# Two of the three matmuls of w_up's split product joined into one of 512 columns, and their halves added by VectorE

## The chip, the cores and the metric

The kernel runs on one core of a Trainium2 chip. The time is the device time of one execution in microseconds; a lower one is better. The runs before the change gave 347.18, 345.4 and 346.83 us, median 346.83. One more execution was profiled: it took 347.6 us, and every row below is from it.

## What is computed

One layer of a decoder with 256 tokens and 1024 features, in fp32: a norm, one projection to q, k and v, two groups of attention heads, an output projection with a residual, then the squared-relu MLP that the change touches, then a gated embedding and a last norm. Cut to what matters here:

```python
D_MODEL, SEQ, D_FF = 1024, 256, 4 * 1024

hn = rmsnorm(h, g_mlp[i])
h = h + jnp.square(jax.nn.relu(hn @ w_up[i])) @ w_down[i]     # w_up (1024, 4096), w_down (4096, 1024)
gate = jax.nn.sigmoid(rmsnorm(h, g_ple[i]) @ w_ple_gate[i] + b_ple_gate[i])
h = h + gate * (p[i] @ w_ple_proj[i])
```

## The kernel before

**Split products.** Each large product is done in fp32r, a format that TensorE takes at the rate of one column per cycle, with both operands split in two: hi is the operand rounded to fp32r by ScalarE (`ACTIVATE Copy`), lo is the operand less hi, by VectorE. A product a·b is then three matmuls into the same PSUM bank, hi·hi, hi·lo and lo·hi. The helper `mm3` (lines 149 to 153) issues them: L151 hi·hi, L152 stationary hi with moving lo or the other way round, L153 the last. Since `mm3` is used everywhere, the lines L151 to L153 carry most of the program's matmuls; the tiles in a row tell the stage: `ps<-hhi,hi` and `ps<-hlo,hi` are the up projection (activations h hi and lo, weights hi and lo), `ps<-hi,u` and `ps<-lo,u` the down projection (u are the activations of the MLP), `ps<-hi,p` the embedding.

**Units.** The program is a list of units, each with its weights (two slabs of 1 MB) and its steps. `run_units` (L109) issues the loads two units ahead on SP's queue, and in the steps of one unit the splits of the next unit's weights: eight pieces of 512 columns for w_up (L75 ScalarE hi, L76 VectorE lo, which also multiply by the norm's gain) and four of 1024 columns for w_down (L83, L84). The scheduler of the language then sets the order of each engine's queue.

**The MLP.** Up unit u (`up_steps`, L588) makes 512 of the 4096 hidden features for all 256 tokens: four blocks c of 128 features, each a sum over eight k of 128 input features. Stationary is a 128x128 block of the weights, moving are the 256 tokens, so one (c, k) is three matmuls of 256 columns, and a unit has 32 of these steps, 96 matmuls. Down unit u (`dn_steps`, L627) multiplies the 512 hidden features with 512 rows of w_down: 16 steps, 48 matmuls of 512 columns, summed over all eight units in four PSUM banks that stay held from the first to the last. The order is up 0, embedding, up 1, down 0, up 2, down 1, ..., up 7, down 6, down 7. Up unit 0 goes over the first four k for all blocks and then over the last four, because the features of its second half are transposed late; the others go block by block.

**The evacuation** of an up block (`act`, L576): relu out of PSUM on ScalarE (L581), the square on GpSimd (L583), hi on ScalarE (L585), lo on VectorE (L586). It works on two blocks (512 columns, one bank) at a time, in unit 0 on one (256 columns).

**The activations.** `act_pair` (L164) gives a tile for hi and one for lo, each with 8 k of 256 tokens; `to_features` (L515) fills them from transposes: hi by ScalarE (L523), lo by VectorE (L524).

Of the kernel before, what the change touches and what calls it, by code (L numbers as in the profile page):

```python
# [10 lines left out]
F32 = mybir.dt.float32  # L11
F32R = mybir.dt.float32r
BF16 = mybir.dt.bfloat16
AF = mybir.ActivationFunctionType
ALU = mybir.AluOpType
PSUM = bass.MemoryType.PSUM

P = 128
S = 256
DM = 1024  # L20
KT = DM // P
# [11 lines left out]
def block_kernel(ctx: ExitStack, tc: tile.TileContext, a: dict):  # L33
    nc = tc.nc

    outer = ctx.enter_context(tc.tile_pool(name="outer", bufs=1))
# [6 lines left out]
    def bank():  # L43
        n_ps[0] += 1
        return psum.tile([P, 512], F32, tag="ps", name=f"ps{n_ps[0]}")
# [103 lines left out]
    def mm3(ps, lhs, rhs, start, stop):  # L149

        nc.tensor.matmul(ps, lhs[0], rhs[0], start=start, stop=False)  # L151
        nc.tensor.matmul(ps, lhs[0], rhs[1], start=False, stop=False)  # L152
        last_mm[0] = nc.tensor.matmul(ps, lhs[1], rhs[0], start=False, stop=stop)  # L153

    last_mm = [None]
# [6 lines left out]
        nc.tensor.matmul(wps[:, :P], warm, warm, start=True, stop=True)  # L162

    def act_pair(name):  # L164
        hi = outer.tile([P, KT, S], F32R, tag="aThi", name=name + "hi")
        lo = outer.tile([P, KT, S], F32R, tag="aTlo", name=name + "lo")
        return hi, lo

    h_sb = outer.tile([P, 2, DM], F32, name="h_sb")
    stat = outer.tile([P, 64], F32, name="stat")  # L170
# [23 lines left out]

    xT = ap.tile([P, KT, S], F32, tag="xy", name="xT")
    aT = act_pair("x")
    x_rows = lambda k0, k1: xT[:, k0:k1] if k0 else head[:, 4 * KT :].unsqueeze(1)

# [340 lines left out]
    def alloc_aT2():  # L539
        state["aT2"] = act_pair("h")  # L540
# [6 lines left out]
    aT2 = Lazy("aT2")  # L547
# [13 lines left out]
    uT = {}  # L561

    def open_mlp():
        attn_pool.__exit__(None, None, None)
        mp["p"] = ctx.enter_context(tc.tile_pool(name="mlp", bufs=1))
        m = mp["p"]
        mp["ple"] = m.tile([P, 2, DM], F32, name="ple")
        mp["bg"] = m.tile([P, 2, DM], F32, name="bg")
        nc.sync.dma_start(mp["bg"], bass.AP(tensor=a["bg"].tensor, offset=a["bg"].offset, ap=[[0, P], [DM, 2], [1, DM]]))
        pT = m.tile([P, 2, S], F32, name="pTin")  # L570
        nc.sync.dma_start(pT, a["pT"])
        mp["p2"] = [m.tile([P, 2, S], F32R, name=f"p2{i}") for i in range(2)]
        nc.scalar.activation(mp["p2"][0], pT, AF.Copy)
        nc.vector.tensor_tensor(mp["p2"][1], pT, mp["p2"][0].bitcast(F32), op=ALU.subtract)

    def act(u, q, ps, c):  # L576

        m = mp["p"]
        w = c * S
        r = m.tile([P, w], F32, tag=f"r{c}", name="r", bufs=2)  # L580
        nc.scalar.activation(r, ps[:, :w], AF.Relu)  # L581
        sq = m.tile([P, w], F32, tag=f"sq{c}", name="sq", bufs=2)
        nc.gpsimd.tensor_tensor(sq, r, r, op=ALU.mult)  # L583
        o = [t.rearrange("p c s -> p (c s)")[:, q * S : q * S + w] for t in uT[u]]
        nc.scalar.activation(o[0], sq, AF.Copy)  # L585
        nc.vector.tensor_tensor(o[1], sq, o[0].bitcast(F32), op=ALU.subtract)  # L586

    def up_steps(u):  # L588
        def steps():
            if u == 0:  # L590
                open_mlp()
            uT[u] = [mp["p"].tile([P, 4, S], F32R, tag=f"u{n}", name="u", bufs=3) for n in ("hi", "lo")]

            def one(ps, c, k):
                s = slabs_up[u][k // 4]
                col = slice(c * P, (c + 1) * P)
                mm3(ps, (s.hi[:, k % 4, col], s.lo[:, k % 4, col]), (aT2[0][:, k], aT2[1][:, k]), k == 0, k == KT - 1)

            if u == 0:
                b = [bank() for _ in range(4)]  # L600
                for kk in range(2):
                    for c in range(4):
                        for k in range(4 * kk, 4 * kk + 4):
                            one(b[c][:, :S], c, k)
                            yield
                        if kk:
                            act(u, c, b[c], 1)
            else:
                for cc in range(2):
                    ps = bank()  # L610
                    for c in (2 * cc, 2 * cc + 1):
                        for k in range(KT):
                            one(ps[:, (c % 2) * S : (c % 2 + 1) * S], c, k)
                            yield
                    act(u, 2 * cc, ps, 2)
        return steps

    dn = {}
# [8 lines left out]
    def dn_steps(u):  # L627
        def steps():
            if u == 0:
                dn["ps"] = {(t, n): bank() for t in range(2) for n in range(2)}  # L630

            def one(t, n, c):
                s = slabs_dn[u][c // 2]
                tok, col = slice(t * P, (t + 1) * P), slice(n * 512, (n + 1) * 512)
                mm3(dn["ps"][t, n], (uT[u][0][:, c, tok], uT[u][1][:, c, tok]),
                    (s.hi[:, c % 2, col], s.lo[:, c % 2, col]), u == 0 and c == 0, u == NU - 1 and c == 3)

            if u < NU - 1:
                for c in range(4):
                    for t in range(2):  # L640
                        for n in range(2):
                            one(t, n, c)
                            yield
                return
            state["aT2"] = act_pair("g")
            for t in range(2):
                for n in range(2):
                    for c in range(4):
                        one(t, n, c)
                        yield  # L650
                    col = slice(n * 512, (n + 1) * 512)
                    nc.vector.scalar_tensor_tensor(h_sb[:, t, col], dn["ps"][t, n], dn["r2"][:, t : t + 1],
                                                   h_sb[:, t, col], op0=ALU.mult, op1=ALU.add)
                    defer(3, lambda t=t, n=n: (to_features(aT2, t, n), row_sum(gsum, t, n)))
        return steps
# [145 lines left out]
```

## Time and profile before

| | |
|---|---|
| median of three runs | 346.83 us (345.4 to 347.18) |
| profiled execution | 347.6 us |
| its span, first to last instruction | 345.8 us |
| mean granted clock of TensorE | 0.982 of 2.4 GHz |
| busy: TensorE, VectorE, ScalarE, GpSimd | 96%, 63%, 58%, 21% of the span |
| moved by DMA | 60.87 MB, 176 GB/s |

Matmuls overlap in the records: one of 256 columns is listed with 283 ns, while the next one starts 120 ns after it. What TensorE needs for one is therefore read as the distance of start times. Busy shares are averages over the whole program; the stretches by stage are among the rows below. Where the order of a queue is shown, an engine's instructions stand in their sequence, with the semaphores that they wait for and no times.

### The profile page before, as it was taken

Reading aid. Unit: us, or ns where it says so; the run is one execution under the profiler, and the core shown is the slowest. Engines: PE = TensorE matmul, PEld = TensorE weight load, DVE = VectorE, ACT = ScalarE, POOL = GpSimd, SP = SyncE. Lnnn points to the kernel's source line nnn. Section 1 sums busy time; section 2 is a strip of 40 time slices with the busy share of each in tenths; the row PEclk is TensorE's granted clock in tenths of the full one; section 3 lists DMA queues with packets and bytes.
Section 4 is the critical chain, followed back from the end, with each engine's and each line's share of the span. In section 5 each row is a group of like instructions: output and inputs, shape, how many; then the busy total and the mean of one; then the engine's idle time right before and its main releaser. Section 6 shows DMA issues by size and latency. Waiting matters only on the chain.

```text
span 345.8 us, 5641 instructions
## 1 busy us (share of the span) xinstructions
PE 333.2 (96%) x2188; PEld 298.9 (86%) x2188; DVE 216.8 (63%) x380; ACT 199.8 (58%) x378; POOL 74.1 (21%) x103
## 2 busy tenths in 40 slices
PE   8899899999999999999999999999999999999990
PEld 8699779899877889898998988989989899888890
DVE  4789948687837769537537275292553843758563
ACT  6786838677664668728255374373652825458431
POOL 0025563455214001311020110110201102000443
PEclk9999969999999999999999999999999999999996
DMA  7998951404444369653727618357194463700011
GB/s 193 372 401 289 316 187 53 160 33 159 163 170 159 112 236 321 206 213 115 261 116 248 237 46 320 123 173 263 51 327 159 136 242 110 243 2 1 2 62 61
DMA packets 10971, 60.87 MB, mean 176 GB/s; under 512 B 1216, under 2 KB 1984, under 8 KB 4416
## 3 DMA queue, kind: packets, MB, share of 16 engines
q1 hardware_dynamic: 10944, 60.51, 49.4%
q8 instruction: 17, 0.28, 0.4%
q14 instruction: 10, 0.08, 0.1%
HBM read 59.46 MB, written 1.05 MB: 175 GB/s over the span
## 4 chain that ended last, share of the span: by engine, by line
PE 92%; DMA 2%; POOL 2%; DVE 1%; SPq 1%; ACT 0%; issue 0%; POOLq 0%; DVEq 0%
PE ps L151 29%; PE ps L152 28%; PE ps L153 28%; DMA raw<-in_w_in 2%; PE ps L328 2%; PE ps L371 2%; PE ps L359 2%; PE ps L519 1%; POOL pb L349 1%; SPq L208 1%; PE ps L372 1%; POOL bias L318 1%; DVE lo L76 0%; POOL bias L316 0%; PE ps L271 0%
## 5 line engine op out<-in xcount | busy, mean ns | idle before, releaser
L76 DVE SCALAR_TENSOR_TENSOR lo<-raw,head,hi 128x512 fp32r<-128x512 f32 (+2 forms) x137 | 105.0, 813 | 24.9 <-ACT hi L75 24.6
L75 ACT ACTIVATE hi<-raw,head 128x512 fp32r<-128x512 f32 (+2 forms) x137 | 92.7, 733 | 25.2 <-PE ps L152 11.1
L151 PE MATMUL ps<-hhi,hi 128*128 128x256 f32 x256 | 72.6, 283 | 0.0
L153 PE MATMUL ps<-hhi,lo 128*128 128x256 f32 x256 | 72.5, 283 | 0.0
L152 PE MATMUL ps<-hlo,hi 128*128 128x256 f32 x256 | 72.4, 283 | 0.0
L84 DVE TENSOR_TENSOR lo<-raw,hi 128x1024 fp32r<-128x1024 f32 x34 | 41.5, 1254 | 28.1 <-ACT hi L83 28.0
L583 POOL TENSOR_TENSOR sq<-r 128x512 f32<-128x512 f32 (+1 forms) x18 | 19.9, 1108 | 141.8 <-ACT r L581 141.8
L151 PE MATMUL ps<-hi,u 128*128 128x512 f32 x128 | 50.2, 392 | 0.0
L83 ACT ACTIVATE hi<-raw 128x1024 fp32r<-128x1024 f32 x34 | 34.3, 1052 | 27.2 <-PE ps L153 25.5
L152 PE MATMUL ps<-lo,u 128*128 128x512 f32 x128 | 49.9, 390 | 0.0
L153 PE MATMUL ps<-hi,u 128*128 128x512 f32 x128 | 49.8, 389 | 0.0
L152 PEld LDWEIGHTS ps<-hlo,hi 128*128 128x128 f32 x256 | 49.1, 192 | 0.3
L151 PEld LDWEIGHTS ps<-hhi,hi 128*128 128x128 f32 x256 | 49.1, 192 | 0.3
L153 PEld LDWEIGHTS ps<-hhi,lo 128*128 128x128 f32 x256 | 49.1, 192 | 0.0
L151 PE MATMUL ps<-xhi,hi 128*128 128x256 f32 x128 | 38.7, 303 | 0.0
L152 PE MATMUL ps<-xlo,hi 128*128 128x256 f32 x128 | 36.9, 289 | 0.0
L153 PE MATMUL ps<-xhi,lo 128*128 128x256 f32 x128 | 36.7, 289 | 0.0
L586 DVE TENSOR_TENSOR u<-sq,u 128x512 fp32r<-128x512 f32 (+1 forms) x18 | 11.7, 650 | 34.0 <-ACT u L585 34.0
L153 PEld LDWEIGHTS ps<-hi,u 128*128 128x128 f32 x128 | 24.0, 188 | 5.1
L151 PEld LDWEIGHTS ps<-hi,u 128*128 128x128 f32 x128 | 24.1, 188 | 4.7
L152 PEld LDWEIGHTS ps<-lo,u 128*128 128x128 f32 x128 | 24.1, 188 | 4.7
L151 PEld LDWEIGHTS ps<-xhi,hi 128*128 128x128 f32 x128 | 25.2, 197 | 1.5 <-issue 0.7
(128 smaller groups left out, 531.7 us busy)
## 6 DMA issues: line engine op xcount, KB each, us to landing
raw<-in_w_up SPq DMA_DIRECT2D x16, 1024.0 KB, 5.1
raw<-in_w_down SPq DMA_DIRECT2D x16, 1024.0 KB, 4.8
raw<-in_w_in SPq DMA_DIRECT2D x8, 1024.0 KB, 7.2
raw<-in_w_out SPq DMA_DIRECT2D x4, 1024.0 KB, 4.9
raw<-in_w_gate SPq DMA_DIRECT2D x4, 1024.0 KB, 5.1
raw<-in_w_in SPq DMA_DIRECT2D x4, 512.0 KB, 8.8
raw<-in_w_in SPq DMA_DIRECT2D x7, 256.0 KB, 7.0
h_sb<-in_x SPq DMA_DIRECT2D x1, 1024.0 KB, 7.4
```

The lines of the kernel that those rows point to most:

```text
L75: nc.scalar.activation(h, r, AF.Copy, scale=sc)
L76: nc.vector.scalar_tensor_tensor(l, r, sc, h.bitcast(F32), op0=ALU.mult, op1=ALU.subtract)
L83: nc.scalar.activation(h, r, AF.Copy)
L84: nc.vector.tensor_tensor(l, r, h.bitcast(F32), op=ALU.subtract)
L151: nc.tensor.matmul(ps, lhs[0], rhs[0], start=start, stop=False)
L152: nc.tensor.matmul(ps, lhs[0], rhs[1], start=False, stop=False)
L153: last_mm[0] = nc.tensor.matmul(ps, lhs[1], rhs[0], start=False, stop=stop)
L328: last_mm[0] = nc.tensor.matmul(ps[h][:, c : c + w], d["q"][a_][r, q0 : q0 + P], d["k"][b_][r, :w], start=i == 0, stop=i == 2)
L359: nc.tensor.transpose(ps[:, c * P : (c + 1) * P], d["p"][:, h, c * P : (c + 1) * P], ident)
L371: nc.tensor.matmul(o[:, :S], v[:, 0, cols], d["pT"][h][:, :S], start=True, stop=False)
L583: nc.gpsimd.tensor_tensor(sq, r, r, op=ALU.mult)
L586: nc.vector.tensor_tensor(o[1], sq, o[0].bitcast(F32), op=ALU.subtract)
```

## The change

The two tiles of hi and lo become one tile in which, for each k, the 256 tokens of hi are followed by the 256 of lo; hi and lo are views of it, and a third view has both as 512 columns. A step of an up unit is now two matmuls: the weights' hi with the activations' hi and lo in one matmul of 512 columns over a whole PSUM bank, and the weights' lo with the activations' hi, 256 columns, added into the second half of the bank. The first half of the bank then holds hi·hi and the second half hi·lo and lo·hi. Each block has its bank, so an up unit uses four.

The evacuation goes block by block in all units: ScalarE copies the second half out of PSUM, VectorE adds the first half to it, VectorE does the squared relu in one operation (maximum with 0, times the value), ScalarE makes hi and VectorE lo. GpSimd has no part in it any more.

```diff
     def act_pair(name):
-        hi = outer.tile([P, KT, S], F32R, tag="aThi", name=name + "hi")
-        lo = outer.tile([P, KT, S], F32R, tag="aTlo", name=name + "lo")
-        return hi, lo
+        both = outer.tile([P, KT, 2, S], F32R, tag="aT", name=name)
+        return both[:, :, 0], both[:, :, 1], both.rearrange("p k h s -> p k (h s)")
...
-    def act(u, q, ps, c):
+    def act(u, q, ps):
         m = mp["p"]
-        w = c * S
-        r = m.tile([P, w], F32, tag=f"r{c}", name="r", bufs=2)
-        nc.scalar.activation(r, ps[:, :w], AF.Relu)
-        sq = m.tile([P, w], F32, tag=f"sq{c}", name="sq", bufs=2)
-        nc.gpsimd.tensor_tensor(sq, r, r, op=ALU.mult)
-        o = [t.rearrange("p c s -> p (c s)")[:, q * S : q * S + w] for t in uT[u]]
-        nc.scalar.activation(o[0], sq, AF.Copy)
-        nc.vector.tensor_tensor(o[1], sq, o[0].bitcast(F32), op=ALU.subtract)
+        b = m.tile([P, S], F32, tag="r", name="r", bufs=3)
+        nc.scalar.copy(b, ps[:, S:])
+        z = m.tile([P, S], F32, tag="z0", name="z0", bufs=3)
+        nc.vector.tensor_tensor(z, ps[:, :S], b, op=ALU.add)
+        sq = m.tile([P, S], F32, tag="sq", name="sq", bufs=3)
+        nc.vector.scalar_tensor_tensor(sq, z, 0.0, z, op0=ALU.max, op1=ALU.mult)
+        hi, lo = (t[:, q] for t in uT[u])
+        nc.scalar.activation(hi, sq, AF.Copy)
+        nc.vector.tensor_tensor(lo, sq, hi.bitcast(F32), op=ALU.subtract)
...
             def one(ps, c, k):
                 s = slabs_up[u][k // 4]
                 col = slice(c * P, (c + 1) * P)
-                mm3(ps, (s.hi[:, k % 4, col], s.lo[:, k % 4, col]), (aT2[0][:, k], aT2[1][:, k]), k == 0, k == KT - 1)
...
+                nc.tensor.matmul(ps, s.hi[:, k % 4, col], aT2[2][:, k], start=k == 0, stop=False)
+                last_mm[0] = nc.tensor.matmul(ps[:, S:], s.lo[:, k % 4, col], aT2[0][:, k],
+                                              start=False, stop=k == KT - 1)
+
+            b = [None] * 4
+            for ks in (range(4), range(4, 8)) if u == 0 else (range(8),):
+                for c in range(4):
+                    if ks[0] == 0:
+                        b[c] = bank()
+                    for k in ks:
+                        one(b[c], c, k)
+                        yield
+                    if ks[-1] == KT - 1:
+                        act(u, c, b[c])
```

TensorE at the start of up unit 2, before (h is the activations, hi and lo behind the comma the weights):

```order
L151 MATMUL ps_2019<-hhi,hi 128x256 [waits Activation_49]
L152 MATMUL ps_2019<-hlo,hi 128x256
L153 MATMUL ps_2019<-hhi,lo 128x256 [waits DVE_49]
L151 MATMUL ps_2019<-hhi,hi 128x256 [waits Activation_49]
L152 MATMUL ps_2019<-hlo,hi 128x256
L153 MATMUL ps_2019<-hhi,lo 128x256 [waits DVE_49]
```

and now:

```order
L598 MATMUL ps_1983<-h,hi 128x512 [waits DVE_49,Activation_49]
L599 MATMUL ps_1983<-h,lo 128x256 [waits DVE_49]
L598 MATMUL ps_1983<-h,hi 128x512 [waits Activation_49]
L599 MATMUL ps_1983<-h,lo 128x256 [waits DVE_49]
L598 MATMUL ps_1983<-h,hi 128x512 [waits Activation_49]
```

Three matmuls of a step became two; the wide one waits for ScalarE's hi of the weights, the narrow one for VectorE's lo, as before. VectorE from the splits for down unit 1 (L84) over up unit 2 to the splits for up unit 3 (L76), before:

```order
L84 TENSOR_TENSOR lo<-raw,hi 128x1024 [waits DMAHW5_49,Activation_49]
L84 TENSOR_TENSOR lo<-raw,hi 128x1024 [waits Activation_49]
L586 TENSOR_TENSOR u<-sq,u 128x512 [waits Activation_49]
L76 SCALAR_TENSOR_TENSOR lo<-raw,head,hi 128x512 [waits DMAHW6_49,PE_49,Activation_49]
L76 SCALAR_TENSOR_TENSOR lo<-raw,head,hi 128x512 [waits Activation_49] x3
L76 SCALAR_TENSOR_TENSOR lo<-raw,head,hi 128x512 [waits DMAHW7_49,PE_49,Activation_49]
L586 TENSOR_TENSOR u<-sq,u 128x512 [waits Activation_49]
L76 SCALAR_TENSOR_TENSOR lo<-raw,head,hi 128x512 [waits Activation_49] x3
```

and now, for the same place, up to the first splits for up unit 3 (z is the sum of the two halves, r the copied half, sq the square, u the lo of the hidden features):

```order
L84 TENSOR_TENSOR lo<-raw,hi 128x1024 [waits DMAHW5_49,Activation_49]
L84 TENSOR_TENSOR lo<-raw,hi 128x1024 [waits Activation_49]
L581 TENSOR_TENSOR z_2008<-ps_1983,r 128x256 [waits Activation_49]
L583 SCALAR_TENSOR_TENSOR sq<-z_2008 128x256 [waits DVE_49]
L586 TENSOR_TENSOR u<-sq,u 128x256 [waits Activation_49]
L581 TENSOR_TENSOR z_2037<-ps_2014,r 128x256 [waits Activation_49]
L583 SCALAR_TENSOR_TENSOR sq<-z_2037 128x256 [waits DVE_49]
L586 TENSOR_TENSOR u<-sq,u 128x256 [waits Activation_49]
L581 TENSOR_TENSOR z_2064<-ps_2043,r 128x256 [waits Activation_49]
L583 SCALAR_TENSOR_TENSOR sq<-z_2064 128x256 [waits DVE_49]
L76 SCALAR_TENSOR_TENSOR lo<-raw,head,hi 128x512 [waits DMAHW6_49,PE_49,Activation_49]
L586 TENSOR_TENSOR u<-sq,u 128x256 [waits Activation_49]
```

Three operations of 256 columns stand now where each half of a subtraction of 512 stood; all four splits of the down weights are still ahead of the first block. Behind this piece, between the splits for up unit 3, the last blocks' operations follow:

```order
L76 SCALAR_TENSOR_TENSOR lo<-raw,head,hi 128x512 [waits Activation_49]
L581 TENSOR_TENSOR z_2089<-ps_2070,r 128x256 [waits Activation_49]
L76 SCALAR_TENSOR_TENSOR lo<-raw,head,hi 128x512 [waits Activation_49]
L583 SCALAR_TENSOR_TENSOR sq<-z_2089 128x256 [waits DVE_49]
L76 SCALAR_TENSOR_TENSOR lo<-raw,head,hi 128x512 [waits Activation_49]
L76 SCALAR_TENSOR_TENSOR lo<-raw,head,hi 128x512 [waits DMAHW7_49,PE_49,Activation_49]
L586 TENSOR_TENSOR u<-sq,u 128x256 [waits Activation_49]
L76 SCALAR_TENSOR_TENSOR lo<-raw,head,hi 128x512
L76 SCALAR_TENSOR_TENSOR lo<-raw,head,hi 128x512 [waits Activation_49] x2
```

The last block's addition and square stand between the eight splits; its lo and that of the block before it do too.

## Rows read from the trace of the kernel before

**Rows 1.** The page: busy time by engine, and the chain that ended last.
```profile
PE 333.2 (96%) x2188; PEld 298.9 (86%) x2188; DVE 216.8 (63%) x380; ACT 199.8 (58%) x378; POOL 74.1 (21%) x103
...
PE 92%; DMA 2%; POOL 2%; DVE 1%; SPq 1%; ACT 0%; issue 0%; POOLq 0%; DVEq 0%
```

**Rows 2.** Windows: up unit 1, down unit 0 (columns in the first line).
```profile
core 0: us, PE busy (x) PEld busy (x) DVE busy (x) ACT busy (x) POOL busy (x), PEclk, DMA share, GB/s
...
145.60:157.10 11.50, 11.50 (x97) 11.48 (x96) 3.63 (x4) 5.06 (x9) 1.04 (x1) 1.00 0.54 182
157.10:168.00 10.90, 10.90 (x50) 9.04 (x49) 8.32 (x11) 6.81 (x11) 1.22 (x1) 1.00 0.62 203
```

**Rows 3.** TensorE's timeline at unit edges: start us, us, engine line operation out<-in.
```profile
145.39 0.39 PE L153 MATMUL ps<-hi,p 128*128 128x512 f32 x1
145.61 0.28 PE L151 MATMUL ps<-hhi,hi 128*128 128x256 f32 x1
145.73 0.28 PE L152 MATMUL ps<-hlo,hi 128*128 128x256 f32 x1
...
157.01 0.28 PE L153 MATMUL ps<-hhi,lo 128*128 128x256 f32 x1
157.13 0.40 PE L151 MATMUL ps<-hi,u 128*128 128x512 f32 x1
...
168.03 0.28 PE L151 MATMUL ps<-hhi,hi 128*128 128x256 f32 x1
```

**Rows 4.** Groups by line, up projection's matmul and weight load: xcount | busy, mean ns.
```profile
L151 PE MATMUL ps<-hhi,hi 128*128 128x256 f32 x256 | 72.6, 283 | 0.0
...
L151 PEld LDWEIGHTS ps<-hhi,hi 128*128 128x128 f32 x256 | 49.1, 192 | 0.3
```

**Rows 5.** Groups by line, shapes apart: evacuation, splits, nearest operations of 256 columns.
```profile
L76 DVE SCALAR_TENSOR_TENSOR lo<-raw,head,hi 128x512 fp32r<-128x512 f32 x127 | 94.2, 788 | 21.2 <-ACT hi L75 20.9
L75 ACT ACTIVATE hi<-raw,head 128x512 fp32r<-128x512 f32 x127 | 83.1, 711 | 25.2 <-PE ps L152 11.1 <-PE ps L153 10.9 <-DMA raw<-in_w_in 3.2
L84 DVE TENSOR_TENSOR lo<-raw,hi 128x1024 fp32r<-128x1024 f32 x34 | 41.5, 1254 | 28.1 <-ACT hi L83 28.0
L83 ACT ACTIVATE hi<-raw 128x1024 fp32r<-128x1024 f32 x34 | 34.3, 1052 | 27.2 <-PE ps L153 25.5 <-PE ps L152 1.8
L586 DVE TENSOR_TENSOR u<-sq,u 128x512 fp32r<-128x512 f32 x14 | 9.6, 686 | 32.9 <-ACT u L585 32.9
L299 DVE TENSOR_TENSOR q<-ps,rb 128x256 f32<-128x256 f32 x8 | 3.3, 419 | 5.6 <-PE ps L153 5.5
L586 DVE TENSOR_TENSOR u<-sq,u 128x256 fp32r<-128x256 f32 x4 | 2.1, 524 | 1.2 <-ACT u L585 1.2
L697 DVE SCALAR_TENSOR_TENSOR z<-ps,stat,bg 128x256 f32<-128x256 f32 x4 | 1.9, 481 | 1.2 <-PE ps L153 1.2
L585 ACT ACTIVATE u<-sq 128x256 fp32r<-128x256 f32 x4 | 1.7, 419 | 2.5 <-POOL sq L583 2.5
L581 ACT ACTIVATE r<-ps 128x256 f32<-128x256 f32 x4 | 1.5, 364 | 0.0
```

**Rows 6.** VectorE's timeline, the last three splits for up unit 2.
```profile
161.24 2.07 DVE L76 SCALAR_TENSOR_TENSOR lo<-raw,head,hi 128x512 fp32r<-128x512 f32 x3
```

**Rows 7.** Timeline, TensorE then VectorE: up unit 0 begins, its features' lo arrive.
```profile
127.77 0.60 PE L519 MATMUL ps<-ident,h_sb 128*128 128x128 f32 x4
128.12 0.36 PE L151 MATMUL ps<-hhi,hi 128*128 128x256 f32 x1
...
125.84 0.69 DVE L524 TENSOR_TENSOR hlo<-ps,hhi 128x512 fp32r<-128x512 f32 x1 [0.32 <-ACT hhi L523]
...
129.50 0.68 DVE L524 TENSOR_TENSOR hlo<-ps,hhi 128x512 fp32r<-128x512 f32 x1
...
132.06 0.69 DVE L524 TENSOR_TENSOR hlo<-ps,hhi 128x512 fp32r<-128x512 f32 x1
```

More of the change, by code (lines that the diff above doesn't have):

```diff
@@ L596, in one @@
                 col = slice(c * P, (c + 1) * P)
-                mm3(ps, (s.hi[:, k % 4, col], s.lo[:, k % 4, col]), (aT2[0][:, k], aT2[1][:, k]), k == 0, k == KT - 1)
[L599 to L615, printed above, removed]
+                nc.tensor.matmul(ps, s.hi[:, k % 4, col], aT2[2][:, k], start=k == 0, stop=False)
[11 more added lines that the diff above has]
+                        act(u, c, b[c])
         return steps
```

## The prediction

> **What bounds the kernel now.** I read the page first, then the windows by stage, then TensorE's timeline at the edges of the units, and last the prices of single operations. On the page TensorE is busy 96% of the span, VectorE 63%, ScalarE 58%, and the chain that ended last runs through TensorE for 92% [rows 1]. In the stretches of the up and down projections TensorE's busy time equals the length of the stretch and the granted clock is 1.00, the 2.4 GHz level, while VectorE is busy for 3.6 of 11.5 us in an up unit and 8.3 of 10.9 us in a down unit [rows 2]. TensorE waits for nobody there, so what an up unit costs is what its matmuls cost TensorE, one after another.
>
> TensorE's price is read from start times, since the durations on the page overlap. Up unit 1 starts at 145.61 and the down unit behind it at 157.13: 11.52 us for 96 matmuls of 256 columns, 0.1200 each. The down unit runs to 168.03: 10.90 us for 48 matmuls of 512 columns, 0.2271 each [rows 3]. At 2.4 GHz, 256 columns are 106.7 ns and 512 are 213.3 ns, so a matmul together with its weight load carries 13.3 ns beside 256 columns and 13.8 ns beside 512. It does not grow with the columns: it is paid once per matmul.
>
> **The change part by part.** *Matmuls.* A step (one column block of 128, one k) was three matmuls of 256 columns, 3 x 0.1200 = 0.3600 us. It becomes one of 512 and one of 256, 0.2271 + 0.1200 = 0.3471. The columns stay 768; one weight load and one matmul go. That is 0.0129 us per step. The stage has 8 units x 4 blocks x 8 k = 256 steps, which agrees with the 256 matmuls of each of the three lines [rows 4]. 256 x 0.0129 = 3.30 us, all on the path, since nothing else ends last there. The trace does not show a stream that alternates the two widths, but it shows both joints: at 145.39 a 512 is followed by a 256 after 0.22, which is followed by the next after 0.12, and at 157.01 a 256 is followed by a 512 after 0.12 [rows 3]. Each matmul keeps the pitch of its own width whatever its neighbour is. Bounds: if the mixed step kept 0.3600 the gain is 0; if the wide matmul also hid the 13.3 ns of the narrow one, the step would be 0.3338 and the gain 256 x 0.0262 = 6.7 us. I take 3.3, where both joints lie.
>
> A rule that speaks against this stands in the Trainium skill, "TensorE: Matmul & The Clock Gate", section "Back-to-back issue gap": a warm matmul in isolation takes its columns at 2.4 GHz plus about 2.5 ns. By it one matmul less per step would give 256 x 2.5 ns, an estimate of 0.6 us; the 13.3 and 13.8 ns above are what this trace shows, and I keep those.
>
> *The evacuation, VectorE.* Per pair of one up and one down unit (22.42 us) VectorE did four subtractions of 1024 columns at 1.254, eight weight splits at 0.788 and two subtractions at 0.686 [rows 5]: 5.02 + 6.30 + 1.37 = 12.69 us. Now each of four blocks has an addition out of PSUM, a squared relu and a subtraction, all of 256 columns. Nearest rows: 0.419 for a tensor-tensor operation (a multiplication) with one operand in PSUM, 0.481 for a scalar-tensor-tensor, 0.524 for the subtraction itself [rows 5]. The fused squared relu with both operands in SBUF is not in the trace; I take 0.481, the nearest in form, with 0.419 below and 0.788 above (the scalar-tensor-tensor of twice the columns, L76). 4 x (0.419 + 0.481 + 0.524) = 5.70, so 17.0 us of the new period of 22.0. The cover is there: TensorE would have to wait only once VectorE's work no longer fits in the period.
>
> *The evacuation, ScalarE and GpSimd.* ScalarE's splits are 4 x 1.052 + 8 x 0.711 = 9.90 us per period; a copy of 256 columns out of PSUM should be near the old relu's 0.364 and the hi copy is 0.419 [rows 5], so it comes to 9.90 + 4 x 0.783 = 13.0 of 22.0. GpSimd loses its squares; it was busy for 21% of the span and ends nothing on the chain but 2% [rows 1], so nothing is gained on the path there.
>
> *The new waits.* ScalarE now waits for two VectorE operations between its copy and its hi copy, where it waited for GpSimd. Behind it in its queue stand the weight splits, in front of all of which TensorE sits one unit later. In the old trace the last of the eight splits made during down unit 0 ended at 161.24 + 2.07 = 163.31 [rows 6], and up unit 2 starts at 168.03 [rows 3], so the splits are 4.7 us early. Between those eight splits the new order puts 2 subtractions, one addition and one square where one subtraction of 0.686 stood: 1.95 - 0.69 = 1.3 us more. The splits of the down units (1024 columns) stay in one row ahead of the first block's addition, as the order shows. The u tiles themselves are read a whole down unit or more later (10.9 us at the least, for unit 7), against a chain of 0.364 + 0.419 + 0.481 + 0.419 + 0.524 = 2.2 us. PSUM: each up unit takes four banks where it took two, and the down units hold the other four; a bank is asked for again about 22 us after its block ended, and is free after the copy and the addition.
>
> *The pair of hi and lo in one tile.* The first matmul of an up unit now needs lo as well as hi. For up unit 0 that counts: the features it starts with have their lo ready at 125.84 + 0.69 = 126.53, the unit starts at 128.12 [rows 7]: 1.6 us of room. Its second half needs the last lo, ready at 132.06 + 0.69 = 132.75; sixteen steps of 0.347 put it at 133.7, without the transposes that come between [rows 7]. The queues of DMA issues are the same, and their transfers used 0.54 to 0.62 of the engines in these units [rows 2]; 2% less time for them costs nothing.
>
> Sum: -3.3 us. Against the profiled execution's 347.6 us (span 345.8, with 1.8 outside) that is 344.3. The median of the three runs shown is 346.83, 0.8 below that execution, so 343.5.
>
> **The rivals.** *The mixed step costs what the three did.* Then the 13 ns belong to something that stays, for instance the switch of weights under a narrow matmul, and only move. For it: no stream of this mix is in the trace, and the record of a weight load lasts 192 ns on average [rows 4], well over a narrow matmul's pitch. Against it: the two joints, and the down units, where the same cost sits beside twice the columns. Time 346.8. The skill's rule above would land within 0.6 us of it.
>
> *VectorE becomes the bound (slower).* VectorE gets 4.3 us more per period. Its pieces leave 22.0 - 11.3 = 10.7 us for four blocks, so the point from which it decides is 2.67 us per block, against 1.42 by the rows [rows 5]. At 1.0 us for each of the three operations the period would be 11.3 + 12.0 = 23.3 instead of 22.42: 0.9 x 7 periods = +6 us, 353. Against it: even three operations at 0.788, the price of twice the columns, are 2.4 us.
>
> *The joined tile makes the first matmul of up unit 0 wait further.* If it waited for the lo of the third group of features, ready at 129.50 + 0.68 = 130.18 [rows 7], TensorE would lose 2.1 us at 128.12 and the sum would be -1.2: 345.6.
>
> **How the numbers follow.** A measurement of this kernel can tell about 0.5% (1.7 us) from no change, so faster means below 345.1. The forecast has 0.77 (its own range 342.6 to 344.6, from half the spread of the three runs, 0.9 us); the mixed step at the old price 0.13 and the joined tile 0.03, both "within 0.5%", 0.16; VectorE as the bound 0.07, slower. The lower end, 342.0, takes some of the second bound of the step (6.7 us would be 340.1); the upper end, 346.4, reaches into the unchanged case and leaves out the slower one.
>
> **What would show it.** Right: in the changed profile an up unit lasts 32 x 0.347 = 11.1 us and the next down unit 10.9, the distance from up unit to up unit falls from 22.42 to 22.0, the line of the wide matmul has 256 records and so has the narrow one, TensorE's busy time still fills every stretch of the MLP, VectorE's share rises to some 73% (216.8 us and eight times 4.3, over 342) and GpSimd's falls. Wrong: an up unit still of 11.5 us (the cost stays), an idle TensorE at the head of an up unit released by a weight split (VectorE is the bound), or an idle one at the head of up unit 0 released by VectorE's lo (the joined tile).

## The result, and the profile after

| | before | after |
|---|---|---|
| median of 12 runs | 346.49 us (345.12 to 347.59) | 344.94 us (342.88 to 346.24) |
| ratio | | 0.9943, 95% interval 0.9921 to 0.9965 |
| profiled execution, its span | 347.6, 345.8 | 342.88, 341.1 |

The kernel is faster by 0.57% (0.35 to 0.79%): 1.6 us by the medians, where 3.3 were forecast. The time lies in the stated range, which is wide enough to hold half the forecast gain. The two profiled executions differ by 4.7 us, and that is not the change either: it has to be taken apart by stage first.

The page after, busy time and chain, beside [rows 1]:

```profile
PE 328.0 (96%) x1932; PEld 282.4 (83%) x1932; DVE 237.3 (70%) x458; ACT 203.3 (60%) x406; POOL 54.0 (16%) x85
...
PE 93%; POOL 2%; DMA 1%; DVE 1%; SPq 0%; ACT 0%; issue 0%; POOLq 0%; DVEq 0%
```

TensorE still makes the chain; 256 matmuls are gone. Now the stretches: first the kernel before in windows of the attention stage, then the kernel after (columns as in [rows 2]):

```profile
40.00:44.00 4.00, 1.99 (x20) 1.71 (x19) 4.00 (x8) 2.66 (x6) 4.00 (x5) 0.92 1.00 387
44.00:48.00 4.00, 3.67 (x18) 3.27 (x17) 2.48 (x12) 2.23 (x9) 3.33 (x6) 0.50 0.48 133
48.00:52.00 4.00, 4.00 (x27) 3.33 (x26) 0.72 (x3) 0.58 (x2) 1.73 (x5) 0.73 0.49 199
...
43.00:44.00 1.00, 0.42 (x2) 0.42 (x3) 1.00 (x3) 0.00 (x0) 1.00 (x2) 0.68 0.84 352
44.00:50.00 6.00, 5.67 (x28) 4.86 (x28) 2.48 (x12) 2.23 (x9) 5.05 (x10) 0.50 0.62 214
50.00:51.00 1.00, 1.00 (x11) 0.74 (x8) 0.00 (x0) 0.25 (x1) 0.00 (x0) 0.91 0.10 41
```

```profile
40.00:44.00 4.00, 1.31 (x10) 0.87 (x9) 4.00 (x10) 2.23 (x4) 3.90 (x5) 1.00 0.83 320
44.00:48.00 4.00, 4.00 (x34) 3.56 (x35) 1.64 (x7) 2.21 (x10) 3.32 (x6) 1.00 0.55 172
48.00:52.00 4.00, 4.00 (x40) 3.79 (x39) 3.60 (x8) 3.43 (x8) 0.98 (x3) 1.00 0.29 117
```

In both executions TensorE stands idle for two of the four microseconds from 40 on (2.01 us in one piece), waiting for GpSimd's probabilities. In the first one the granted clock then falls to 0.50, the 1.2 GHz level, from within the window 43 to 44 until shortly after 50; in the second one, after a little more idling, it stays at 1.00. The matmuls behind the wait start at 43.58 in the first and at 42.74 in the second, 0.84 us apart; the projection's first matmul behind the product with the values starts at 50.62 and at 47.40, 3.22 apart. So 0.84 us were there before the clock fell, and 2.4 came with it. Up unit 0 starts at 128.12 [rows 7] and now at 124.90, still 3.22 apart.

That stage is not touched by the change, and this distance is luck, as the other traces show. The mean clocks of the runs overlap: 0.982 to 0.995 in 33 runs of the kernel before, 0.984 to 0.992 in 12 of the kernel after. All the experiments below share the joined tile and the stages ahead of the MLP; in their traces and the one after, twelve in all, up unit 0 starts between 124.60 (e10) and 128.59 us (e8), and in e2's, whose clock fell in the same way, at 127.98. The rest of the 4.7 us, 1.5, is the change, and the medians say the same. It shows directly as the distance from the first matmul of up unit 0 to the last of the down units, first before, then after (the start of up unit 0 before is in [rows 7]):

```profile
314.60 0.39 PE L153 MATMUL ps<-hi,u 128*128 128x512 f32 x1
```

```profile
309.89 0.40 PE L153 MATMUL ps<-hi,u 128*128 128x512 f32 x1
```

That is 314.60 - 128.12 = 186.48 us before and 309.89 - 124.90 = 184.99 after: 1.49 us.

TensorE's timeline after, at the edges of up unit 1, down unit 0 and up unit 2, and inside a block, beside [rows 3]:

```profile
124.90 0.48 PE L598 MATMUL ps<-h,hi 128*128 128x512 f32 x1
...
142.20 0.39 PE L598 MATMUL ps<-h,hi 128*128 128x512 f32 x1
...
153.49 0.40 PE L151 MATMUL ps<-hi,u 128*128 128x512 f32 x1
...
164.44 0.39 PE L598 MATMUL ps<-h,hi 128*128 128x512 f32 x1
...
170.08 0.40 PE L598 MATMUL ps<-h,hi 128*128 128x512 f32 x1
170.31 0.28 PE L599 MATMUL ps<-h,lo 128*128 128x256 f32 x1
170.43 0.40 PE L598 MATMUL ps<-h,hi 128*128 128x512 f32 x1
170.67 0.28 PE L599 MATMUL ps<-h,lo 128*128 128x256 f32 x1
170.79 0.40 PE L598 MATMUL ps<-h,hi 128*128 128x512 f32 x1
...
175.73 0.40 PE L151 MATMUL ps<-hi,u 128*128 128x512 f32 x1
```

Up unit 1 lasts 153.49 - 142.20 = 11.29 us, up unit 2 the same, where 11.1 were forecast; 32 steps of 0.3528 and not 0.3471. Two steps inside the block, from 170.08 to 170.79, take 0.71. The down unit behind takes 10.95 where it took 10.90, by edges that are rounded to 0.01. The window shows no idle TensorE and a full clock, so the missing time is inside the stream of matmuls:

```profile
142.20:153.40 11.20, 11.20 (x65) 9.70 (x64) 6.14 (x11) 5.67 (x11) 0.00 (x0) 1.00 0.55 189
153.50:164.40 10.90, 10.90 (x50) 9.01 (x49) 8.51 (x14) 6.63 (x11) 0.00 (x0) 1.00 0.59 201
```

The new operations, grouped by line with shapes apart, beside [rows 5]:

```profile
L583 DVE SCALAR_TENSOR_TENSOR sq<-z 128x256 f32<-128x256 f32 x32 | 13.5, 423 | 0.8
L581 DVE TENSOR_TENSOR z<-ps,r 128x256 f32<-128x256 f32 x32 | 13.4, 420 | 13.4 <-ACT r L579 13.4
L586 DVE TENSOR_TENSOR u<-sq,u 128x256 fp32r<-128x256 f32 x32 | 13.4, 422 | 6.8 <-ACT u L585 6.8
L579 ACT COPY r<-ps 128x256 f32<-128x256 f32 x32 | 11.7, 367 | 19.7 <-PE ps L599 19.6
```

A block costs VectorE 1.27 us (forecast 1.42), and the splits are as early as they were: VectorE's last three for up unit 2 end at 159.65, 4.8 us ahead of the unit (4.7 before, [rows 3, 6]):

```profile
157.58 2.07 DVE L76 SCALAR_TENSOR_TENSOR lo<-raw,head,hi 128x512 fp32r<-128x512 f32 x3
```

### The profile page after: what moved, and what is told of

Same layout as the page of the kernel before. It is cut to its first block, busy times and chain, and to the rows that moved or that the text cites. A ratio compares the mean times of both kernels' runs of the same rounds, so it can differ in the third digit from the quotient of the medians.

```text
span 341.1 us, 5223 instructions
## 1 busy us (share of the span) xinstructions
PE 328.0 (96%) x1932; PEld 282.4 (83%) x1932; DVE 237.3 (70%) x458; ACT 203.3 (60%) x406; POOL 54.0 (16%) x85
## 4 chain that ended last, share of the span: by engine, by line
PE 93%; POOL 2%; DMA 1%; DVE 1%; SPq 0%; ACT 0%; issue 0%; POOLq 0%; DVEq 0%
PE ps L151 21%; PE ps L153 20%; PE ps L152 20%; PE ps L598 18%; PE ps L599 9%; PE ps L327 2%; PE ps L370 2%; PE ps L358 2%; DMA raw<-in_w_in 1%; PE ps L518 1%; POOL pb L348 1%; PE ps L371 1%; POOL bias L317 1%; POOL bias L315 0%; PE ps L270 0%
## 5 line engine op out<-in xcount | busy, mean ns | idle before, releaser
L76 DVE SCALAR_TENSOR_TENSOR lo<-raw,head,hi 128x512 fp32r<-128x512 f32 (+2 forms) x137 | 102.9, 790 | 17.7 <-ACT hi L75 17.4
L598 PE MATMUL ps<-h,hi 128*128 128x512 f32 x256 | 90.9, 399 | 0.0
L599 PE MATMUL ps<-h,lo 128*128 128x256 f32 x256 | 71.9, 281 | 0.0
L84 DVE TENSOR_TENSOR lo<-raw,hi 128x1024 fp32r<-128x1024 f32 x34 | 40.5, 1222 | 26.5 <-ACT hi L83 26.5
L598 PEld LDWEIGHTS ps<-h,hi 128*128 128x128 f32 x256 | 48.1, 188 | 11.8
L599 PEld LDWEIGHTS ps<-h,lo 128*128 128x128 f32 x256 | 48.4, 189 | 0.3
L183 POOL TENSOR_TENSOR stat<-stat,mhalf 128x2 f32<-128x2 f32 x5 | 4.4, 873 | 228.9 <-DVE stat L182 228.9
L151 PE MATMUL ps<-x,hi 128*128 128x256 f32 x128 | 37.9, 297 | 1.4 <-ACT hi L75 1.4
L152 PE MATMUL ps<-x,hi 128*128 128x256 f32 x128 | 36.1, 282 | 0.0
L153 PE MATMUL ps<-x,lo 128*128 128x256 f32 x128 | 35.9, 283 | 0.0
L151 PEld LDWEIGHTS ps<-x,hi 128*128 128x128 f32 x128 | 24.3, 190 | 3.1 <-ACT hi L75 1.6
L152 PEld LDWEIGHTS ps<-x,hi 128*128 128x128 f32 x128 | 24.4, 190 | 0.3
L153 PEld LDWEIGHTS ps<-x,lo 128*128 128x128 f32 x128 | 24.2, 190 | 0.3 <-DVE lo L76 0.3
L579 ACT COPY r<-ps 128x256 f32<-128x256 f32 x32 | 11.7, 367 | 19.7 <-PE ps L599 19.6
```

The lines of the kernel that those rows point to most:

```text
L76: nc.vector.scalar_tensor_tensor(l, r, sc, h.bitcast(F32), op0=ALU.mult, op1=ALU.subtract)
L84: nc.vector.tensor_tensor(l, r, h.bitcast(F32), op=ALU.subtract)
L579: nc.scalar.copy(b, ps[:, S:])
L598: nc.tensor.matmul(ps, s.hi[:, k % 4, col], aT2[2][:, k], start=k == 0, stop=False)
L599: last_mm[0] = nc.tensor.matmul(ps[:, S:], s.lo[:, k % 4, col], aT2[0][:, k], start=False, stop=k == KT - 1)
```

## The experiments

The question was why a mixed step takes 0.353. Inside a down unit, behind its first block, the start times give 0.2267 per wide matmul (and so does e6 below, 14.50 us for 64), so the additive price of a mixed step is 0.2267 + 0.1200 = 0.3467 and that of an up unit 11.09. All edits are to the changed kernel's `one` or to the loop around it, and are shown shortened.

**Grouping the widths (e1), and the evacuation alone (e2).**

```diff
-    for k in ks:
-        one(b[c], c, k)        # wide, narrow
+    for k in ks:  wide(b[c], c, k)
+    for k in ks:  narrow(b[c], c, k)
```

> The changed kernel with the matmuls of each block grouped: first the eight wide ones (512 columns), then the eight narrow ones (256), so that the width changes twice per block of 16 matmuls and not 16 times. The changed kernel's up unit lasts 11.29 us where the prediction had 11.1. Theory 'switch' (a wide matmul behind a narrow one costs some 7 ns more): the up unit falls to 11.1 to 11.2 us and the time by 0.8 to 1.5 us against the changed kernel, to about 343.7. Theory 'width' (a wide matmul over this operand costs 0.2337 us whatever stands beside it) and theory 'company' (VectorE's and ScalarE's new work slows TensorE's reads): 11.29 us as it is, no change against 344.9.

```diff
-    nc.tensor.matmul(ps, s.hi[...], aT2[2][:, k], ...)
+    nc.tensor.matmul(ps[:, :S], s.hi[...], aT2[0][:, k], ...)
+    nc.tensor.matmul(ps[:, S:], s.hi[...], aT2[1][:, k], ...)
     nc.tensor.matmul(ps[:, S:], s.lo[...], aT2[0][:, k], ...)
```

> The changed kernel's joined tile, four banks and whole evacuation, with three matmuls of 256 columns per step as before (hi.hi into the first half of the bank, hi.lo and lo.hi into the second). It prices the evacuation alone. Theories 'switch' and 'width': step 0.3600 us, up unit 11.52 us, time as before the change, 346.5. Theory 'company': TensorE is slower than that, up unit 11.7 us or more, time 348 or more.

e1: 344.09 us, ratio to before 0.992 (0.9896 to 0.9945, which overlaps the changed kernel's). e2: 346.57, ratio 0.9994 (0.9979 to 1.0010). The edges of up unit 2, first e1, then e2:

```profile
167.18 0.39 PE L599 MATMUL ps<-h,hi 128*128 128x512 f32 x1
...
178.32 0.40 PE L151 MATMUL ps<-hi,u 128*128 128x512 f32 x1
...
189.23 0.39 PE L599 MATMUL ps<-h,hi 128*128 128x512 f32 x1
```

```profile
167.89 0.28 PE L599 MATMUL ps<-h,hi 128*128 128x256 f32 x1
...
179.40 0.40 PE L151 MATMUL ps<-hi,u 128*128 128x512 f32 x1
```

With the widths grouped the same matmuls take 11.14 us, 0.05 above the additive price, and the down unit 10.91: 'width' and 'company' have fallen. With three narrow ones and the whole new evacuation the unit takes 11.51, as before the change, and the distance from the first matmul of up unit 0 to the last down matmul is 314.45 - 127.98 = 186.47, also as before: the additions and squares on VectorE cost nothing on the path.

**Pairs (e3), the half of the bank (e4).** e3 uses e1's loop over two k at a time; e4:

```diff
-    nc.tensor.matmul(ps[:, S:], s.lo[...], aT2[0][:, k], ...)
+    nc.tensor.matmul(ps[:, :S], s.lo[...], aT2[0][:, k], ...)
```

> The changed kernel with matmuls in the order wide, wide, narrow, narrow over two k at a time: half as many changes of width. 'switch': the 7 ns per step are halved, step 0.350, up unit 11.20 us. 'width' and 'company': 11.29 us.

> The changed kernel with the narrow matmul (weights' lo) added into the first half of the bank in place of the second; the sum of the halves is the same. Theory 'bank' (the narrow matmul adds to columns that the wide one has only just written, and has to wait): up unit falls to 11.1 us. 'switch', 'width' and 'company': 11.29 us.

e3: 343.86 us (one run), up unit 2 from 166.61 to 177.75. e4: 343.43 (one run), 164.98 to 176.27:

```profile
164.98 0.39 PE L598 MATMUL ps<-h,hi 128*128 128x512 f32 x1
...
176.27 0.40 PE L151 MATMUL ps<-hi,u 128*128 128x512 f32 x1
```

e4 keeps 11.29: the bank's half has no part in it. e3 has 11.14, not the 11.20 expected of half as many changes: four times the changes of width of e1 cost no more than e1's. So 'switch', a fixed price for each wide matmul behind a narrow one, was wrong in its form, though right that it is the order.

**What the second matmul is (e5 to e8).** The second matmul becomes 384 columns wide, 512, 128, or takes the weights' hi:

```diff
-    nc.tensor.matmul(ps[:, S:], s.lo[...], aT2[0][:, k], ...)
+    nc.tensor.matmul(ps[:, :384], s.lo[...], aT2[2][:, k, :384], ...)        # e5
+    nc.tensor.matmul(ps, s.lo[...], aT2[2][:, k], ...)                       # e6
+    nc.tensor.matmul(ps[:, S : S + P], s.lo[...], aT2[0][:, k, :P], ...)     # e7
+    nc.tensor.matmul(ps[:, S:], s.hi[...], aT2[0][:, k], ...)                # e8
```

> The changed kernel with the second matmul widened to 384 columns (weights' lo with the activations' hi and half of their lo, added from column 0 of the bank; the added product is of the size of the rounding). By additive prices a step is 0.2267 + (384 + 32)/2400 = 0.400 us, an up unit 12.80. 'load window' (the extra 7 ns arises because the weights of the wide matmul must be loaded beside only 256 columns): 12.80. 'alternation of widths' (any narrower matmul standing alone between wide ones): 0.407, 13.0.

> The changed kernel with the second matmul 512 columns wide too (weights' lo with the activations' hi and lo; the added product is of the size of the rounding). Stationary operands still alternate between the hi and the lo slab. 'alternation of widths' and 'load window': a step is 2 x 0.2267 = 0.4533, an up unit 14.5 us. 'alternation of weights' (each change between the hi and the lo slab costs): 0.460 or more, 14.7.

> The changed kernel with the second matmul cut to 128 columns, which leaves out the product of the weights' lo for the second 128 tokens. If the 13 ns are paid once per matmul: a step is 0.2267 + (128 + 32)/2400 = 0.293 us, an up unit 9.39. If a narrow matmul is really as long as the load of the next weights (a floor of some 0.120 us under any width): 0.347 or more, 11.1 to 11.3.

> The changed kernel with the narrow matmul taking the weights' hi again in place of lo, which leaves out the product of the weights' lo and adds hi.hi a second time. Widths alternate, the stationary slab does not. 'alternation of weights': up unit 11.1 us. 'alternation of widths' and 'load window': 11.29.

One run each; the times follow the units (358.84, 369.98, 341.31, 346.60 us). The edges of up unit 2 in e5, then e6, then e7:

```profile
170.35 0.39 PE L598 MATMUL ps<-h,hi 128*128 128x512 f32 x1
...
183.35 0.40 PE L151 MATMUL ps<-hi,u 128*128 128x512 f32 x1
```

```profile
172.61 0.39 PE L598 MATMUL ps<-h,hi 128*128 128x512 f32 x1
...
187.11 0.39 PE L151 MATMUL ps<-hi,u 128*128 128x512 f32 x1
```

```profile
165.43 0.39 PE L598 MATMUL ps<-h,hi 128*128 128x512 f32 x1
...
175.92 0.44 PE L598 MATMUL ps<-h,hi 128*128 128x512 f32 x1
176.20 0.22 PE L599 MATMUL ps<-h,lo 128*128 128x128 f32 x1
176.26 0.44 PE L151 MATMUL ps<-hi,u 128*128 128x512 f32 x1
```

e5: 13.00 us, 0.20 over the additive 12.80, 6 ns per step: 384 columns alone between wide ones pay like 256, so 'load window' has fallen as it was stated, for 256 columns only. e6: 14.50, the additive price exactly: equal widths pay nothing, and that the slab changes with every matmul costs nothing. e8, with one slab, keeps 11.29 (168.12 to 179.41), which says the same from the other side. e7 fell between its two cases: 10.83, a step of 0.338, where the fixed price gives 0.293. Taking 128 columns from the narrow matmul saves 14 ns of the 53 that they are at 2.4 GHz. The wide one now begins 0.06 us after the narrow one and is recorded with 0.44 us in place of 0.40. TensorE's weight loads in the same stretch of e7:

```profile
175.86 0.19 PEld L598 LDWEIGHTS ps<-h,hi 128*128 128x128 f32 x1
175.97 0.19 PEld L599 LDWEIGHTS ps<-h,lo 128*128 128x128 f32 x1
```

The two loads begin 0.11 us apart, although the matmul between them would need only 0.067 by the additive price, and 0.2267 + 0.11 is close to the step of 0.338. So next to a matmul that short the load of the wide one's weights probably sets the pace; no run here varies the load alone, so this is not shown.

**Which of the two pays (e10, e11), and the pairs timed (e9).**

```diff
 # e10: every second k with two matmuls of 256 columns for the weights' hi
+    if k % 2:  hi.hi into ps[:, :S], hi.lo into ps[:, S:]
+    else:      wide
     narrow
 # e11: every second k with a second matmul of 512 columns
     wide
+    if k % 2 == 0:  nc.tensor.matmul(ps, s.lo[...], aT2[2][:, k], ...)
+    else:           narrow
```

> Every second step does the weights' hi with two matmuls of 256 columns, so a wide matmul stands between four narrow ones: wide, narrow, narrow, narrow, narrow. By additive prices two steps are 0.2267 + 4 x 0.12 = 0.7067, an up unit 11.31 us. 'lone wide' (a wide matmul with narrow ones on both sides costs 7 ns more): 0.7137, 11.42 us. 'strict alternation' or 'lone narrow': 11.31.

> Every second step does the weights' lo 512 columns wide too (the added product is of the size of the rounding), so a narrow matmul stands between three wide ones: wide, wide, wide, narrow. By additive prices two steps are 3 x 0.2267 + 0.12 = 0.800, an up unit 12.80 us. 'lone narrow' (a narrow matmul with wide ones on both sides costs 7 ns more): 0.807, 12.91 us. 'strict alternation' or 'lone wide': 12.80.

> The changed kernel with the matmuls in the order wide, wide, narrow, narrow, now timed. In the look before, its up unit lasted 11.14 us and its down unit 10.89, against 11.29 and 10.94 in the changed kernel and 11.52 and 10.90 before the change. Over the stage that is 8 x 0.15 + 8 x 0.05 = 1.6 us less than the changed kernel, 3.1 less than before: about 343.4 us. If the time follows something else than these units, it stays near 345.

Up unit 2 in e10, in e11, and in e9:

```profile
164.23 0.39 PE L599 MATMUL ps<-h,hi 128*128 128x512 f32 x1
...
175.59 0.40 PE L151 MATMUL ps<-hi,u 128*128 128x512 f32 x1
```

```profile
169.88 0.39 PE L598 MATMUL ps<-h,hi 128*128 128x512 f32 x1
...
182.84 0.40 PE L151 MATMUL ps<-hi,u 128*128 128x512 f32 x1
```

```profile
165.41 0.39 PE L599 MATMUL ps<-h,hi 128*128 128x512 f32 x1
...
176.55 0.40 PE L151 MATMUL ps<-hi,u 128*128 128x512 f32 x1
...
187.44 0.39 PE L599 MATMUL ps<-h,hi 128*128 128x512 f32 x1
```

e10 (342.93 us, one run) takes 11.36, between its two cases: 3 ns over the additive price for each of its 16 lone wide matmuls. e11 (358.20, one run) takes 12.96, 10 ns over for each of its 16 lone narrow ones, more than expected. Neither unit is at its additive price, so 'strict alternation' has fallen too.

The extra, shared out over the changes from narrow to wide, is thus no fixed price: 6 ns in the changed kernel (32 changes in an up unit), 3 in pairs (e9: 11.14 against 11.09, 16 changes) and in e10, 10 in e11, and 13 with eight in a row (e1: 11.14, 4 changes). Pairs and groups of eight win because their changes are cheap or few. The starts also put the extra behind the wide matmuls, not the narrow one: between 170.08 and 170.79 above, the two wide ones take 0.23 and 0.24, the two narrow ones 0.12 each. The kernel before shows it as well. Down unit 0, from 157.13 on [rows 3], stands behind 96 narrow matmuls:

```profile
158.29 0.39 PE L153 MATMUL ps<-hi,u 128*128 128x512 f32 x1
...
159.42 0.39 PE L152 MATMUL ps<-lo,u 128*128 128x512 f32 x1
```

Its first five matmuls take 1.16 us, the next five 1.13, which is 5 x 0.2267. What in TensorE does this stays open. The half of the bank (e4), the slab (e8, e6) and VectorE's work (e2) are excluded. A weight load that has to fit beside the narrow matmul is not wholly excluded: the records of loads last 188 ns on average in e5, longer than the pitch of 384 columns, 173. But equal matmuls of 256 columns, with a shorter pitch still, pay nothing.

e9 gave 343.76 us, ratio to before 0.9917 (0.9892 to 0.9941), with a distance from up unit to up unit of 22.03 (before 22.42, changed kernel 22.23). From the first matmul of up unit 0 to the last down matmul it takes 309.62 - 126.23 = 183.39 us, 1.6 less than the changed kernel and 3.1 less than the kernel before. It is the best version here by the units; by the times alone its interval still overlaps the changed kernel's.

## Why the prediction was right in sign and too large

*Bound.* Right: TensorE fills every stretch of the MLP before and after, and nothing else ends last there.

*The matmuls.* This is the term that was mis-sized. The count was right (256 wide, 256 narrow) and so was the kind of gain, a fixed price for each matmul that goes: e9, with the same matmuls in another order, gains 3.1 us in the stage. The sentence that failed is "Each matmul keeps the pitch of its own width whatever its neighbour is." It was read off single joints at unit edges, at a resolution of 0.01 us, for a difference of 0.007, and neither joint holds the distance behind a wide matmul that follows a narrow one, which is where the extra lies. In a stream that alternates strictly the step is 0.3528 and not 0.3471. 256 x (0.3528 - 0.3467) = 1.6 us, about half of the forecast gain, is the price of the order.

*Not in the sum.* The down unit behind an alternating up unit is longer too. Over six periods, the start of up unit 1 to that of up unit 7 (145.61 to 280.13 before, 142.20 to 275.60 after), the distance from up unit to up unit is 22.42 and 22.23, where 22.0 was forecast. That is 0.19 for a pair, though the up unit alone gives 0.22 to 0.23: the down unit takes back 0.03 to 0.04. Seven pairs give 1.3 us, and up unit 0, from 12.03 (128.12 to 140.15) to 11.84 (124.90 to 136.74), gives 0.2: the 1.5 of the stage. The first down steps carried a little of the extra before the change; it was averaged into the 0.2271.

*The bounds.* They held: the gain lies between 0 (0.3600) and 6.7 us. The forecast's own range, 342.6 to 344.6, missed by 0.3, though the kernel before ran 0.3 us faster in this comparison (346.49) than in the runs that the forecast started from.

*The rivals.* "The mixed step costs what the three did" lies about as near in its time, but not in its mechanism: the 13 ns went with the matmul, since e9 gains them, and a change of slab costs nothing (e6, e8). What came on top is the order of the widths, which no rival named. The Trainium skill ("TensorE: Matmul & The Clock Gate", "Back-to-back issue gap") gives 2.5 ns beside the columns for a warm matmul in isolation; these streams do not run at that price, but at 13 ns beside 256 and beside 512 columns, in equal widths. VectorE as the bound: excluded, 1.27 us per block against a deciding point of 2.67, and e2 shows no loss. The joined tile: up unit 0 starts with TensorE busy up to it, no wait there.

*The evacuation.* Each 256-column operation of VectorE took 0.42, including the fused square whose price was open (0.423 against 0.481 taken), and VectorE's share rose to 70%, not to 73. GpSimd's absence gave nothing on the path, as forecast.

## What to carry to other kernels

Fewer and wider matmuls save a fixed price each, here 13 ns, but a stream that alternates strictly between widths gave half of it back: put wide and narrow ones at least two in a row. A difference of a few nanoseconds per instruction is read from the length of a whole unit, never from one joint. Two profiled executions are compared stage by stage, and the stage that the change does not touch is subtracted first.

## What the runs showed of the hardware

- Where one matmul of 256 or 384 columns stands between matmuls of 512, the stream takes 6 to 10 ns more for each than the sum of the prices in equal widths (6 in the changed kernel and e5, 10 in e11). In pairs it is 3 ns for each pair (e9); e6, with equal widths, pays nothing. The extra lies in the distances behind the wide matmuls (0.23 to 0.24 us from 170.08 to 170.79 after the change, where 0.2267 is the price).
- Below 256 columns a matmul between wide ones saves little: 14 ns for 128 columns (e7, 0.338 against 0.353).
- The same wait of TensorE, 2.01 us, ended with some 6.8 us at 1.2 GHz in one execution (the windows 43 to 51 above) and with none in another: 2.4 us of difference, more than the change.
